# Two input column blocks side by side while x arrives, with the squares of x, the constants and eight extra matmuls moved to go with it

## The chip, the cores and the metric

One core of a Trainium2 chip runs the whole program. The time is the device time of one execution in microseconds. Each kernel is run several times; the median counts. A further execution is taken with the hardware profiler; the rows below come from it.

## What is computed

One transformer block on 512 tokens of width 2048, in float32: a norm, one wide input projection, a state-space mixer and a sparse-attention mixer side by side, an output projection, and a gated feed-forward layer of width 5632 with a last norm.

```python
def rmsnorm(x, w):
    xf = xf * lax.rsqrt(jnp.mean(xf * xf, axis=-1, keepdims=True) + NORM_EPS)
    return xf.astype(x.dtype) * w
...
u = rmsnorm(h, attn_norm_w[l])
z, xbc, dt_raw, q, kc, vc, ks, vs, kw, vw, gate_raw = jnp.split(u @ w_in[l], split_at, axis=-1)
y_ssd = ssd_mixer(z, xbc, dt_raw, ...)
y_att = nsa_mixer(q, kc, vc, ks, vs, kw, vw, gate_raw, ...)
h = h + jnp.concatenate([y_ssd, y_att], axis=-1) @ w_out[l]
v = rmsnorm(h, ffn_norm_w[l])
h = h + (jax.nn.silu(v @ w_gate[l]) * (v @ w_up[l])) @ w_down[l]
return rmsnorm(h, final_norm_w)
```

The change concerns the first norm and the first two of the 41 column blocks of `u @ w_in`.

## The kernel before

**Layout.** Everything is held transposed: features lie on the 128 partitions, the 512 tokens along a row. x is 16 row blocks of 128 features (`xt`, KD = 16), each 128 x 512.

**A product of float32 accuracy** is three fast matmuls. Weight and operand are each split into a high part (rounded by a copy on ScalarE) and a low part (the rest, on VectorE); TensorE adds high x high, high x low and low x high into one PSUM bank (lines 254, 255 and 256). For u the high part is ScalarE's copy of x times the norm's gain, and the low part one VectorE operation with two multiplied and subtracted operands (line 1955). The norm's scale, 1/rms of each token, is not in u: it is multiplied in later, when a finished column block is read from PSUM (`rrow`).

**A column block** of the input projection is a `Unit`: 16 row blocks, 48 matmuls of 512 columns into one bank. Its weights come in four transfers of four row blocks each, 256 KB (`subs`). `issue_dma` starts a transfer into one of four `raw` buffers, `issue_split` makes the high part (`whi`, four buffers), `issue_low` the low part (`wlo`, four buffers). `run_unit` runs one block after another, with splits three transfers ahead (LEAD). The banks: two `ps_t` for the first two blocks, two `ps_s` for the next two, two `ps_g` from then on. A block is read out ("evacuated") by VectorE with `rrow`, so none is read before the norm's sums are through; from the seventh block on, a block starts only when the one two before it has been read.

**The start.** SP's queue takes the transfers in order: a weight transfer, x's first row block, the gains (`colc`), then the rest of x with a weight transfer after every second transfer of x, then the constants (`ident` for transposes, `tri`, the large table of masks and rotation angles in `kc`). The squares of x are taken in the same stretch: even row blocks on ScalarE with the sum added up on GpSimd, odd ones squared and added on VectorE; then the two sums are added. `rms_stats` lets TensorE sum over the partitions by four matmuls with ones (line 306), takes the power on GpSimd and spreads the result by four transposes (line 316).

**What sets the order.** Up to the output projection a scheduler orders each engine's instructions by its own simulated timeline, within what the data allow. From the feed-forward layer on the order is written in the program (`manual_schedule`). On the chip every engine takes its list in order and waits on semaphores.

Of the kernel before, what the change touches and what calls it, by code (L numbers as in the profile page):

```python
# [29 lines left out]
LEAD = 3  # L30
# [81 lines left out]
def body(ctx, tc, xT, w_in, w_out, w_gate, w_up, w_down, w1k, w1v, cols, rows, kst, out):  # L112
    nc = tc.nc
    act, dve, pool, pe = nc.scalar, nc.vector, nc.gpsimd, nc.tensor
    sch = Sched()

    def f(ap):
        return ap.bitcast(F32)

    def a_hi(dst, src, scale=1.0):  # L120
        act.activation(dst, src, AF.Copy, scale=scale)  # L121
# [4 lines left out]
    def mul(eng, o, a, b):  # L126
        eng.tensor_tensor(o, a, b, ALU.mult)

    def add(eng, o, a, b):
        eng.tensor_tensor(o, a, b, ALU.add)  # L130
# [20 lines left out]
    def ps_m():  # L151
        return ps("m", 1)
# [30 lines left out]
    subs = []  # L183
# [9 lines left out]
                subs.append((src[:, k:k + n, :], n))  # L193

    st = {"dma": 0, "split": 0, "low": 0}
    raw, hi_t, lo_t = {}, {}, {}

    def issue_dma(upto):
        while st["dma"] <= min(upto, len(subs) - 1):
            i = st["dma"]  # L200
            src, n = subs[i]
            raw[i] = wp.tile([128, KSUB, 128], F32, tag="raw", name="wraw", bufs=4)
            nc.sync.dma_start(raw[i][:, :n, :], src)
            st["dma"] += 1
# [25 lines left out]

    U_LAST = NU + KD + 2

    def run_unit(u):
        if u.pre:
            u.pre()
        if u.need:
            sch.run_until(*u.need)
        n_u = st["unit"] = st.get("unit", 0) + 1
        if n_u > 6:
            sch.run_until(("evac", n_u - 2))  # L240
        p = ps_t() if n_u <= 2 or n_u > U_LAST + 2 else ps_s() if n_u <= 4 or U_LAST < n_u <= U_LAST + 2 else ps_g()
        p = p[:, 0:u.cols[1] - u.cols[0]]
        unit_of[id(p)] = n_u
        for i, k0, n in u.sub:
            issue_low(i)
            for j in range(n):
                if j == 0:
                    issue_split(i + LEAD)
                if j == 2:
                    issue_low(i + LEAD)  # L250
                k = k0 + j
                ah, al = [t[:, u.cols[0]:u.cols[1]] for t in u.rhs(k)]
                with tc.issue_after(R["pv"].ins) if u.late else nullcontext():
                    pe.matmul(p, hi_t[i][:, j, :], ah, start=(k == 0), stop=False)  # L254
                    pe.matmul(p, hi_t[i][:, j, :], al, start=False, stop=False)  # L255
                    pe.matmul(p, lo_t[i][:, j, :], ah, start=False, stop=(k == u.nk - 1))  # L256
                sch.tick()
                if u.hook:
                    u.hook(k)
            del hi_t[i], lo_t[i]  # L260

        def evac():
            yield 1
            yield from u.evac(p)
            assert ("evac", n_u) in sch.flags
            del unit_of[id(p)]
        sch.add(evac())


    colc = cst.tile([128, C_W2 + 4], F32, name="colc")  # L270
    nhalf = colc[:, C_W2:C_W2 + 4]
    ones = cst.tile([128, 128], F32, name="ones")
    ident = cst.tile([128, 128], F32, name="ident")
# [14 lines left out]
    def kcs(a, n):  # L288
        return kc[:, a - K_TRI:a - K_TRI + n]

    tri = kcs(K_TRI, 128)
# [4 lines left out]
    def col(c, n=1):  # L296
        return colc[:, c:c + n]
# [1637 lines left out]

    xs = open_pool("xs")
    xt = xs.tile([128, KD, 512], F32, name="xt")
    issue_dma(0)
    nc.sync.dma_start(xt[:, 0, :], xT[0])
    nc.sync.dma_start(colc[:, 0:C_PE], cols[:, 0:C_PE])  # L1940
    nc.sync.dma_start(xt[:, 1, :], xT[1])
    for k in range(2, KD, 2):
        nc.sync.dma_start(xt[:, k:k + 2, :], xT[k:k + 2].rearrange("k p t -> p k t"))
        if k % 4 == 2:
            issue_dma(k // 4 + 1)
    nc.gpsimd.dma_start(rowc, rows.to_broadcast([128, 48]))
    dve.memset(ones, 1.0)
    act.activation(nhalf, ones[:, 0:4], AF.Copy, scale=-0.5)
    for k in range(KD):
        if k % 4 == 0:  # L1950
            issue_low(k // 4)
        t = xt[:, k, :]
        w = col(C_AN + k)
        a_hi(u_hi[:, k, :], t, scale=w)
        dve.scalar_tensor_tensor(u_lo[:, k, :], t, w, f(u_hi[:, k, :]), op0=ALU.mult, op1=ALU.subtract)
    acc1 = acc2
    accb = xs.tile([128, 512], F32, name="accb")
    for k in range(KD):
        t = xt[:, k, :]
        if k < 2:  # L1960
            act.activation((acc1, accb)[k], t, AF.Square)
        else:
            sq = xs.tile([128, 512], F32, tag=f"sq{k % 2}", name="sq", bufs=2)
            if k % 2:
                mul(dve, sq, t, t)
                add(dve, accb, accb, sq)
            else:
                act.activation(sq, t, AF.Square)
                add(pool, acc1, acc1, sq)
    add(dve, acc1, acc1, accb)  # L1970
    nc.sync.dma_start(ident, kst[:, 0:K_TRI])
    nc.sync.dma_start(tri, kst[:, K_TRI:K_AM])
    close_pool("xs")
    open_pool("kcp")
    open_pool("ssd")
# [4 lines left out]
    first = units[0].evac  # L1980

    def ev_first(p):
        yield from rms_stats(acc1, D, rrow, "r1")
        yield from first(p)
    units[0].evac = ev_first
    for n, u in enumerate(units):
        if n == 4:
            nc.sync.dma_start(kcs(K_AM, NK - K_AM), kst[:, K_AM:NK])
            nc.sync.dma_start(colc[:, C_PE:C_W2], cols[:, C_PE:C_W2])
# [98 lines left out]
```

## Time and profile before

| | us |
|---|---|
| timed runs | 2243.98, 2245.19, 2245.45 (median 2245.19) |
| the profiled execution | 2247.26 |
| its span, first to last instruction | 2245.5 |
| mean granted clock of TensorE | 0.99 |
| DMA | 419.57 MB, 187 GB/s on average |

The span of the profile is cut into windows or listed by instruction; times in it count from its start. A matmul's printed duration overlaps the next matmul's, since they are pipelined: the distance from one start to the next is the cost. PE is TensorE, PEld its weight loads, DVE VectorE, ACT ScalarE, POOL GpSimd, SP the queue that issues most transfers. `ps_t<-u,whi` means: writes a bank `ps_t`, reads u and a weight's high part.

### The profile page before, as it was taken

The numbers are of one execution on the slowest core, as the hardware profiler recorded it, in microseconds if no ns is written. First come the engines' busy times: TensorE is split into PE (matmuls) and PEld (weight loads), VectorE is DVE, ScalarE is ACT, GpSimd is POOL, SyncE is SP. The second block draws the span as 40 slices with busy tenths as digits, with TensorE's granted clock in tenths as the row PEclk, the third lists the DMA queues.
The fourth block names the chain that finished last, engine by engine and source line by source line (L and its number), as shares of the span: only waits on it lengthen the run. The fifth ranks groups of instructions, "written<-read, shape, count | busy, mean of one in ns | idle before, by whom it ended". The sixth has DMA issues, their size and how long they took to land.

```text
span 2245.5 us, 39743 instructions
## 1 busy us (share of the span) xinstructions
PE 2176.5 (97%) x15376; PEld 2028.3 (90%) x15376; DVE 1811.8 (81%) x2912; ACT 1092.1 (49%) x1767; POOL 430.5 (19%) x440
## 2 busy tenths in 40 slices
PE   7999999999999999999999999999999899999996
PEld 5888888888888778999999999999999799999995
DVE  7698777788788777888888888888788887877886
ACT  4564456667666644444444444444444343333353
POOL 2011234333233133000000000000001221112132
PEclk9999999999999999999999999999999999999998
DMA  5222352222435165878788787878876867878775
GB/s 179 91 74 76 115 171 92 88 87 73 153 128 154 54 230 156 247 219 242 215 255 228 227 235 214 251 225 245 229 219 223 327 206 256 252 248 254 218 176 142
DMA packets 153645, 419.57 MB, mean 187 GB/s; under 512 B 16512, under 2 KB 24720, under 8 KB 153456
## 3 DMA queue, kind: packets, MB, share of 16 engines
q1 hardware_dynamic: 99712, 252.63, 32.7%
q0 software_dynamic: 25456, 77.37, 17.7%
q10 hardware_dynamic: 28288, 87.04, 11.1%
q8 instruction: 120, 1.97, 0.4%
q14 instruction: 69, 0.57, 0.1%
HBM read 353.54 MB, written 59.51 MB: 184 GB/s over the span
## 4 chain that ended last, share of the span: by engine, by line
PE 86%; DVE 6%; DMA 4%; issue 2%; ACT 1%; POOL 0%; ACTq 0%; DVEq 0%; POOLq 0%; SPq 0%
PE ps_g L254 8%; PE ps_g L256 8%; PE ps_g L255 8%; PE ps_t L1363 6%; PE ps_g L1363 6%; PE ps_g L1362 6%; PE ps_g L1361 6%; PE ps_t L1361 6%; PE ps_s L1363 6%; PE ps_t L1362 6%; PE ps_s L1361 6%; PE ps_s L1362 6%; DVE R L124 2%; PE ps_v L984 2%; PE ps_t L957 1%
## 5 line engine op out<-in xcount | busy, mean ns | idle before, releaser
L121 ACT ACTIVATE R<-Z 128x1024 fp32r<-128x1024 f32 (+5 forms) x477 | 433.4, 926 | 542.5 <-DVE Z L130 304.8
L124 DVE TENSOR_TENSOR R<-Z,R 128x1024 fp32r<-128x1024 f32 (+5 forms) x371 | 386.2, 1047 | 28.8 <-ACT R L121 22.2
L254 PE MATMUL ps_g<-u,whi 128*128 128x512 f32 x736 | 293.1, 399 | 0.0
L256 PE MATMUL ps_g<-u,wlo 128*128 128x512 f32 x736 | 290.6, 395 | 0.0
L255 PE MATMUL ps_g<-u,whi 128*128 128x512 f32 x736 | 289.4, 393 | 0.2 <-DVE u L124 0.2
L1361 PE MATMUL ps_s<-u,R 128*128 128x256 f32 (+1 forms) x747 | 215.4, 288 | 1.7 <-ACT R L121 1.7
L1362 PE MATMUL ps_s<-u,R 128*128 128x256 f32 (+1 forms) x747 | 214.9, 288 | 0.0
L1361 PE MATMUL ps_g<-u,R 128*128 128x256 f32 (+1 forms) x748 | 213.8, 286 | 0.2 <-ACT R L121 0.2
L1362 PE MATMUL ps_g<-u,R 128*128 128x256 f32 (+1 forms) x748 | 213.2, 285 | 0.0
L1361 PE MATMUL ps_t<-u,R 128*128 128x256 f32 (+1 forms) x705 | 202.0, 287 | 0.2 <-ACT R L121 0.2
L1362 PE MATMUL ps_t<-u,R 128*128 128x256 f32 (+1 forms) x705 | 201.6, 286 | 0.0
L124 DVE TENSOR_TENSOR wlo<-wraw,whi 128x512 fp32r<-128x512 f32 x200 | 158.4, 794 | 52.5 <-ACT whi L121 51.6
L121 ACT ACTIVATE whi<-wraw 128x512 fp32r<-128x512 f32 x200 | 125.3, 627 | 144.0 <-PE ps_g L255 97.4
L1363 PE MATMUL ps_g<-u,R 128*128 128x256 f32 (+1 forms) x620 | 177.9, 287 | 2.3 <-DVE R L124 2.2
L1363 PE MATMUL ps_s<-u,R 128*128 128x256 f32 (+1 forms) x595 | 170.3, 286 | 2.5 <-DVE R L124 2.5
L256 PEld LDWEIGHTS ps_g<-u,wlo 128*128 128x128 f32 x736 | 138.5, 188 | 27.4
L255 PEld LDWEIGHTS ps_g<-u,whi 128*128 128x128 f32 x736 | 138.7, 188 | 26.4 <-DVE u L124 0.5
L254 PEld LDWEIGHTS ps_g<-u,whi 128*128 128x128 f32 x736 | 138.7, 188 | 25.6 <-ACT e L121 0.2
L1361 PEld LDWEIGHTS ps_s<-u,R 128*128 128x128 f32 x747 | 140.5, 188 | 4.1 <-ACT R L121 2.1
L1362 PEld LDWEIGHTS ps_s<-u,R 128*128 128x128 f32 x747 | 141.0, 189 | 2.2
L1361 PEld LDWEIGHTS ps_g<-u,R 128*128 128x128 f32 x748 | 140.7, 188 | 1.8 <-ACT R L121 0.4
L1362 PEld LDWEIGHTS ps_g<-u,R 128*128 128x128 f32 x748 | 141.0, 189 | 1.5
(470 smaller groups left out, 6436.4 us busy)
## 6 DMA issues: line engine op xcount, KB each, us to landing
Z<-in_w_gate SPq DMA_DIRECT2D x95, 512.0 KB, 5.3
Z<-in_w_up SPq DMA_DIRECT2D x93, 512.0 KB, 7.3
wraw<-in_w_in SPq DMA_DIRECT2D x164, 256.0 KB, 3.0
g_d<-A ACTq DMA_DIRECT2D x22, 1792.0 KB, 7.4
Z<-in_w_down SPq DMA_DIRECT2D x59, 384.0 KB, 6.0
u<-g_d ACTq DMA_DIRECT2D x11, 1792.0 KB, 8.7
Z<-in_w_gate POOLq DMA_DIRECT2D x35, 512.0 KB, 7.5
Z<-in_w_up POOLq DMA_DIRECT2D x35, 512.0 KB, 5.6
```

The lines of the kernel that those rows point to most:

```text
L121: act.activation(dst, src, AF.Copy, scale=scale)
L124: eng.tensor_tensor(dst, src, f(hi), ALU.subtract)
L254: pe.matmul(p, hi_t[i][:, j, :], ah, start=(k == 0), stop=False)
L255: pe.matmul(p, hi_t[i][:, j, :], al, start=False, stop=False)
L256: pe.matmul(p, lo_t[i][:, j, :], ah, start=False, stop=(k == u.nk - 1))
L957: pe.transpose(p[:, kb * 128:(kb + 1) * 128], e[:, kb * 128:(kb + 1) * 128], ident)
L984: R["pv"] = pe.matmul(o[:, kb * 128:512], v[:, kb, br, :], rhs, start=False, stop=(br == 1 and kb == 3 and t is tl))
L1361: pe.matmul(q, h[:, k, :], ah, start=(k == 0), stop=False)
L1362: pe.matmul(q, h[:, k, :], al, start=False, stop=False)
L1363: pe.matmul(q, l[:, k, :], ah, start=False, stop=(k == s.blk.n - 1))
```

## The change

It does five things.

1. The first two column blocks run side by side: the weight transfers of the two are taken in turn, and after every four row blocks of x come the 12 matmuls of the one and the 12 of the other. `run_unit` is cut into `start_unit`, `run_sub` and `end_unit` for that; for the other blocks nothing changes in it.
2. The weight transfers are placed between those of x at other points, six of them ahead of x's end instead of four.
3. All squares of x are taken on ScalarE and added up on VectorE into one sum, and both stand behind that engine's last split of u. GpSimd has no part in it.
4. Constants are loaded later, behind the weight transfers issued so far (`issue_after` sets only the order on the queue).
5. Eight matmuls of ones by ones, 128 x 128, go to TensorE ahead of everything; their result is not read.

```diff
-    raw, hi_t, lo_t = {}, {}, {}
+    raw, hi_t, lo_t, raw_dma = {}, {}, {}, []
...
-            nc.sync.dma_start(raw[i][:, :n, :], src)
+            raw_dma.append(nc.sync.dma_start(raw[i][:, :n, :], src))
...
+    def run_unit(u):
+        p, n_u = start_unit(u)
+        for sub in u.sub:
+            run_sub(u, p, sub)
+        end_unit(u, p, n_u)
...
+    pair = units[0:2]
+    subs[0:8] = [subs[4 * (i % 2) + i // 2] for i in range(8)]
+    for a, u in enumerate(pair):
+        u.sub = [(2 * g + a, k, n) for g, (_, k, n) in enumerate(u.sub)]
     issue_dma(0)
     nc.sync.dma_start(xt[:, 0, :], xT[0])
     nc.sync.dma_start(colc[:, 0:C_PE], cols[:, 0:C_PE])
+    issue_dma(1)
     nc.sync.dma_start(xt[:, 1, :], xT[1])
     for k in range(2, KD, 2):
+        if k > 2:
+            issue_dma(k // 2)
         nc.sync.dma_start(xt[:, k:k + 2, :], xT[k:k + 2].rearrange("k p t -> p k t"))
-        if k % 4 == 2:
-            issue_dma(k // 4 + 1)
...
-    for k in range(KD):
-        if k % 4 == 0:
-            issue_low(k // 4)
...
-        a_hi(u_hi[:, k, :], t, scale=w)
-        dve.scalar_tensor_tensor(u_lo[:, k, :], t, w, f(u_hi[:, k, :]), op0=ALU.mult, op1=ALU.subtract)
-    acc1 = acc2
-    accb = xs.tile([128, 512], F32, name="accb")
+    warm = ps_m()
+    for _ in range(8):
+        pe.matmul(warm[:, 0:128], ones, ones, start=True, stop=True)
+    p0 = [start_unit(u) for u in pair]
+    for g in range(4):
+        for k in range(4 * g, 4 * g + 4):
+            if k % 4 < 2:
+                issue_low(2 * g + k % 4)
+            t = xt[:, k, :]
+            w = col(C_AN + k)
+            last_hi = act.activation(u_hi[:, k, :], t, AF.Copy, scale=w)
+            last_lo = dve.scalar_tensor_tensor(u_lo[:, k, :], t, w, f(u_hi[:, k, :]), op0=ALU.mult, op1=ALU.subtract)
+        for u, (p, _) in zip(pair, p0):
+            run_sub(u, p, u.sub[g])
     for k in range(KD):
         t = xt[:, k, :]
-        if k < 2:
-            act.activation((acc1, accb)[k], t, AF.Square)
-        else:
-            sq = xs.tile([128, 512], F32, tag=f"sq{k % 2}", name="sq", bufs=2)
-            if k % 2:
-                mul(dve, sq, t, t)
-                add(dve, accb, accb, sq)
-            else:
-                act.activation(sq, t, AF.Square)
-                add(pool, acc1, acc1, sq)
-    add(dve, acc1, acc1, accb)
-    nc.sync.dma_start(ident, kst[:, 0:K_TRI])
-    nc.sync.dma_start(tri, kst[:, K_TRI:K_AM])
+        with tc.issue_after(last_hi.ins):
+            if k:
+                sq = xs.tile([128, 512], F32, tag=f"sq{k % 2}", name="sq", bufs=2)
+            act.activation(sq if k else acc2, t, AF.Square)
+        with tc.issue_after(last_lo.ins):
+            if k:
+                add(dve, acc2, acc2, sq)
+    with tc.issue_after(raw_dma[-1].ins):
+        nc.sync.dma_start(ident, kst[:, 0:K_TRI])
+        nc.sync.dma_start(tri, kst[:, K_TRI:K_AM])
...
+            with tc.issue_after(raw_dma[-1].ins):
+                nc.sync.dma_start(kcs(K_AM, NK - K_AM), kst[:, K_AM:NK])
+                nc.sync.dma_start(colc[:, C_PE:C_W2], cols[:, C_PE:C_W2])
```

What the scheduler makes of it is seen in three places. The numbers behind the names tell buffers apart.

TensorE in the kernel before, where the second column block (bank `ps_t_301`) first appears, after 36 matmuls of the first (`ps_t_234`):

```order
L256 MATMUL ps_t_234<-u_95,wlo_150 128x512
L254 MATMUL ps_t_234<-u_95,whi_162 128x512
L254 MATMUL ps_t_301<-u_95,whi_247 128x512
L255 MATMUL ps_t_301<-u_95,whi_247 128x512
L255 MATMUL ps_t_234<-u_95,whi_162 128x512
L256 MATMUL ps_t_234<-u_95,wlo_164 128x512
```

TensorE now, from its first instruction (first block `ps_t_139`, second `ps_t_140`):

```order
L1967 MATMUL ps_m_130<-ones_77 128x128 x8
L257 MATMUL ps_t_139<-u_95,whi_141 128x512
L257 MATMUL ps_t_140<-u_95,whi_147 128x512
L258 MATMUL ps_t_139<-u_95,whi_141 128x512
L259 MATMUL ps_t_139<-u_95,wlo_143 128x512
L258 MATMUL ps_t_140<-u_95,whi_147 128x512
L259 MATMUL ps_t_140<-u_95,wlo_149 128x512
```

The second block has moved from the 37th place to the second: both blocks use a row block of x as soon as it is there. The norm's sums (lines 306 before, 316 now) stand after 90 of the 512-column matmuls before and after 151 now.

ScalarE before, around the last split of x and behind it (`u` is a split, `sq` a square, `whi` a weight's high part):

```order
L121 ACTIVATE whi_162<-wraw_115 128x512
L121 ACTIVATE u_95<-xt_100,colc_76 128x512 x2
L1968 ACTIVATE sq_209<-xt_100 128x512
L121 ACTIVATE u_95<-xt_100,colc_76 128x512 x2
L1968 ACTIVATE sq_215<-xt_100 128x512
L121 ACTIVATE whi_247<-wraw_119 128x512
L121 ACTIVATE whi_265<-wraw_152 128x512
```

ScalarE now, at the same place; `whi_219` and `whi_245` are the high parts of the last four row blocks of the two first column blocks:

```order
L1975 ACTIVATE u_95<-xt_100,colc_76 128x512 x2
L121 ACTIVATE whi_201<-wraw_118 128x512
L1975 ACTIVATE u_95<-xt_100,colc_76 128x512 x6
L1984 ACTIVATE acc2_96<-xt_100 128x512
L1984 ACTIVATE sq_326<-xt_100 128x512
L1984 ACTIVATE sq_329<-xt_100 128x512
L1984 ACTIVATE sq_332<-xt_100 128x512
L1984 ACTIVATE sq_335<-xt_100 128x512
L121 ACTIVATE whi_219<-wraw_121 128x512
L121 ACTIVATE whi_245<-wraw_124 128x512
L121 ACTIVATE whi_263<-wraw_211 128x512
```

The squares have moved from between the splits of x to behind them, five of them ahead of the two high parts.

SP's queue before, from its first transfer:

```order
L203 DMA wraw_101<-in_w_in 128x512
L1939 DMA xt_100<-in_xT 128x512
L1940 DMA colc_76<-in_cols 128x116
L1941 DMA xt_100<-in_xT 128x512
L1943 DMA xt_100<-in_xT 128x2x512
L203 DMA wraw_107<-in_w_in 128x512
L1943 DMA xt_100<-in_xT 128x2x512 x2
L203 DMA wraw_111<-in_w_in 128x512
```

SP's queue now:

```order
L203 DMA wraw_101<-in_w_in 128x512
L1954 DMA xt_100<-in_xT 128x512
L1955 DMA colc_76<-in_cols 128x116
L203 DMA wraw_105<-in_w_in 128x512
L1957 DMA xt_100<-in_xT 128x512
L1961 DMA xt_100<-in_xT 128x2x512
L203 DMA wraw_109<-in_w_in 128x512
L1961 DMA xt_100<-in_xT 128x2x512
```

A second weight transfer stands ahead of x's second row block, and weights and x then alternate one to one.

More of the change, by code (lines that the diff above doesn't have):

```diff
@@ L231, in body, with start_unit @@
     U_LAST = NU + KD + 2
-    def run_unit(u):
+    def start_unit(u):
         if u.pre:
@@ L243, in run_unit, with run_sub, end_unit @@
         unit_of[id(p)] = n_u
[L244 to L260, printed above, removed]
+        return p, n_u
+    def run_sub(u, p, sub):
+        i, k0, n = sub
+        issue_low(i)
+        for j in range(n):
+            if j == 0:
+                issue_split(i + LEAD)
+            if j == 2:
+                issue_low(i + LEAD)
+            k = k0 + j
+            ah, al = [t[:, u.cols[0]:u.cols[1]] for t in u.rhs(k)]
+            with tc.issue_after(R["pv"].ins) if u.late else nullcontext():
+                pe.matmul(p, hi_t[i][:, j, :], ah, start=(k == 0), stop=False)
+                pe.matmul(p, hi_t[i][:, j, :], al, start=False, stop=False)
+                pe.matmul(p, lo_t[i][:, j, :], ah, start=False, stop=(k == u.nk - 1))
+            sch.tick()
+            if u.hook:
+                u.hook(k)
+        del hi_t[i], lo_t[i]
+    def end_unit(u, p, n_u):
         def evac():
@@ L1937, in body @@
     xt = xs.tile([128, KD, 512], F32, name="xt")
+    pair = units[0:2]
+    assert [i for u in pair for i, _, _ in u.sub] == list(range(8))
+    subs[0:8] = [subs[4 * (i % 2) + i // 2] for i in range(8)]
+    for a, u in enumerate(pair):
+        u.sub = [(2 * g + a, k, n) for g, (_, k, n) in enumerate(u.sub)]
     issue_dma(0)
@@ L1948, in body @@
     act.activation(nhalf, ones[:, 0:4], AF.Copy, scale=-0.5)
-    for k in range(KD):
-        if k % 4 == 0:
-            issue_low(k // 4)
-        t = xt[:, k, :]
-        w = col(C_AN + k)
-        a_hi(u_hi[:, k, :], t, scale=w)
-        dve.scalar_tensor_tensor(u_lo[:, k, :], t, w, f(u_hi[:, k, :]), op0=ALU.mult, op1=ALU.subtract)
-    acc1 = acc2
-    accb = xs.tile([128, 512], F32, name="accb")
+    warm = ps_m()
[12 more added lines that the diff above has]
+            run_sub(u, p, u.sub[g])
     for k in range(KD):
         t = xt[:, k, :]
-        if k < 2:
-            act.activation((acc1, accb)[k], t, AF.Square)
-        else:
-            sq = xs.tile([128, 512], F32, tag=f"sq{k % 2}", name="sq", bufs=2)
-            if k % 2:
-                mul(dve, sq, t, t)
-                add(dve, accb, accb, sq)
-            else:
-                act.activation(sq, t, AF.Square)
-                add(pool, acc1, acc1, sq)
-    add(dve, acc1, acc1, accb)
-    nc.sync.dma_start(ident, kst[:, 0:K_TRI])
-    nc.sync.dma_start(tri, kst[:, K_TRI:K_AM])
+        with tc.issue_after(last_hi.ins):
[8 more added lines that the diff above has]
+        nc.sync.dma_start(tri, kst[:, K_TRI:K_AM])
     close_pool("xs")
@@ L1982, in ev_first @@
     def ev_first(p):
-        yield from rms_stats(acc1, D, rrow, "r1")
+        yield from rms_stats(acc2, D, rrow, "r1")
         yield from first(p)
     units[0].evac = ev_first
+    for u, (p, n_u) in zip(pair, p0):
+        end_unit(u, p, n_u)
     for n, u in enumerate(units):
         if n == 4:
-            nc.sync.dma_start(kcs(K_AM, NK - K_AM), kst[:, K_AM:NK])
-            nc.sync.dma_start(colc[:, C_PE:C_W2], cols[:, C_PE:C_W2])
+            with tc.issue_after(raw_dma[-1].ins):
+                nc.sync.dma_start(kcs(K_AM, NK - K_AM), kst[:, K_AM:NK])
+                nc.sync.dma_start(colc[:, C_PE:C_W2], cols[:, C_PE:C_W2])
+        if n < 2:
+            continue
         if order.index(first_att) <= n < len(units) - 1:
```

## The prediction

> **What bounds the kernel now.** First the page's busy times, then the first 40 us in windows, then who waited there, then the matmuls one by one.
>
> ```profile
> span 2245.5 us, 39743 instructions
> PE 2176.5 (97%) x15376; PEld 2028.3 (90%) x15376; DVE 1811.8 (81%) x2912; ACT 1092.1 (49%) x1767; POOL 430.5 (19%) x440
> ```
> ```profile
> 0.00:10.00 10.00, 3.07 (x6) 2.10 (x7) 3.85 (x7) 6.43 (x11) 0.93 (x5) 1.00 0.78 245
> 10.00:20.00 10.00, 4.70 (x11) 2.15 (x9) 10.00 (x9) 10.00 (x18) 6.85 (x5) 0.84 1.06 391
> 20.00:30.00 10.00, 8.00 (x20) 5.67 (x21) 10.00 (x13) 3.19 (x7) 2.70 (x2) 0.67 0.21 75
> 30.00:40.00 10.00, 9.70 (x40) 7.30 (x40) 9.09 (x17) 2.57 (x5) 0.00 (x0) 0.98 0.42 135
> ```
> ```profile
> PEld ps_t L255 <- DVE u L1955: 12.2, 9, 3.4
> ```
> TensorE is the bound of the whole kernel (97%). It is not so in the first 34 us: there it starts at most 37 matmuls in 30 us, and its weight loads wait for VectorE's low parts of u (12.2 us in nine waits). VectorE is full from 10 to 30 us. The windows' columns are PE, PEld, DVE, ACT, POOL, granted clock, DMA share, GB/s.
>
> ```profile
> 6.93 0.79 PE L254 MATMUL ps_t<-u,whi 128*128 128x512 f32 x1 [6.93 <-ACT u L121]
> 8.73 0.63 PE L254 MATMUL ps_t<-u,whi 128*128 128x512 f32 x1
> 9.16 0.63 PE L255 MATMUL ps_t<-u,whi 128*128 128x512 f32 x1
> ...
> 35.95 0.39 PE L254 MATMUL ps_t<-u,whi 128*128 128x512 f32 x1
> ...
> 43.20 0.39 PE L256 MATMUL ps_t<-u,wlo 128*128 128x512 f32 x1
> 43.43 0.95 PE L306 MATMUL ps_m<-ones,acc 128*128 128x1 f32 x8
> 44.23 0.48 PE L254 MATMUL ps_t<-u,whi 128*128 128x512 f32 x1
> ...
> 45.69 0.39 PE L254 MATMUL ps_s<-u,whi 128*128 128x512 f32 x1
> ```
> Between 35.95 and 43.20 us stand 32 matmul periods: 0.2266 us each at full clock. At 8.73 and 9.16 they are 0.43 us apart: half clock. The first two column blocks are 2 x 16 x 3 = 96 matmuls; they end where ps_s begins, at 45.69. Without the norm's sums (43.43 to 44.23, 0.80 us), which the change moves behind them, that is 44.89. At the full pace 96 take 21.75 us; from 6.93 they would end at 28.7. So 16.2 us are lost in this stretch, and that is all that can be won there if the first matmul doesn't come earlier.
>
> **What the change does to the stretch.** Durations first: the start's groups of instructions, then three low-part splits beside GpSimd and three after it.
>
> ```profile
> L1955 DVE SCALAR_TENSOR_TENSOR u<-xt,colc,u 128x512 fp32r<-128x512 f32 x16 | 15.4, 996 | 0.6 <-ACT u L121 0.6
> L121 ACT ACTIVATE u<-xt,colc 128x512 fp32r<-128x512 f32 x16 | 10.6, 710 | 0.1
> L130 POOL TENSOR_TENSOR acc<-acc,sq 128x512 f32<-128x512 f32 x7 | 9.6, 1365 | 11.9 <-ACT sq L1968 11.9
> L121 ACT ACTIVATE whi<-wraw 128x512 fp32r<-128x512 f32 x11 | 6.9, 626 | 19.0 <-PE ps_t L255 10.3 <-DMA wraw<-in_w_in 5.2 <-issue 2.0
> L1968 ACT ACTIVATE sq<-xt 128x512 f32<-128x512 f32 x7 | 4.3, 615 | 0.0
> ```
> ```profile
> 18.25 4.10 DVE L1955 SCALAR_TENSOR_TENSOR u<-xt,colc,u 128x512 fp32r<-128x512 f32 x3
> 22.17 1.32 POOL L130 TENSOR_TENSOR acc<-acc,sq 128x512 f32<-128x512 f32 x1 [0.37 <-ACT sq L1968]
> 25.17 2.06 DVE L1955 SCALAR_TENSOR_TENSOR u<-xt,colc,u 128x512 fp32r<-128x512 f32 x3
> 24.57 0.68 DVE L124 TENSOR_TENSOR wlo<-wraw,whi 128x512 fp32r<-128x512 f32 x1
> ```
> Three splits take 4.10 us beside GpSimd's adds and 2.06 us once these are over. The change removes GpSimd's seven adds, and puts VectorE's squares and adds behind the last split. VectorE's 16 splits of u and six of weights then take 16 x 0.69 + 6 x 0.62 = 14.8 us (paces from the last two rows: 2.06/3, and 25.17 - 24.57 plus a little). Fifteen VectorE operations go and fifteen adds come: no more work for it, but later.
>
> ```profile
> 6.15 1.35 ACT L121 ACTIVATE u<-xt,colc 128x512 fp32r<-128x512 f32 x2
> 8.13 1.03 SPq L1943 DMA_DIRECT2D xt<-in_xT  x2
> ```
> ```profile
> xt<-in_xT SPq DMA_DIRECT2D x1, 512.0 KB, 9.6
> ```
> *Transfers.* Weight block, x and gains come first on SP's queue, as before, so the first split starts at 6.15 and the first matmul at 6.93 again. The last x was issued at about 8.8 and landed 9.6 us later, at 18.4, with four weight blocks on the queue ahead of it. Now six are ahead; two more of 0.262 MB at 391 GB/s (row of 10 to 20 us) are 1.3 us: 19.7. The seventh and eighth weight blocks, issued behind all of x, land at 20.4 and 21.1. ScalarE follows x: its last split ends at 21.1, VectorE's at 21.9.
>
> *TensorE.* With two blocks side by side each row block of x feeds 6 matmuls, 1.36 us at full clock, and a row block arrives every 0.8 us (fifteen between about 7.4 and 19.7). So after the first three or four row blocks TensorE is the bound, not the splits. I laid the steps out in the program's order with these durations. If the clock were full from the first matmul, TensorE would wait 1.7 us for data and end the 96 at 30.4. If it stays at half until 13.4 us, almost no wait is left and the end is 31.9; early half clock falls where data is short anyway. I take **31.1**, between the two, against 44.89: **13.8 us gained**, with ends of 14.5 and 13.0.
>
> *Waits on the way.* On ScalarE the fifth block's high part waits for a buffer that TensorE frees after 24 matmuls, at 13 to 16 us, with ten splits of x queued behind it; it is due at 14.3, so they slip by 1.5 us at most, and TensorE has 24 more matmuls to do meanwhile. On SP the fifth block's transfer waits for VectorE's first low part (6.3 us) with x behind it, which is before its turn. One place has no cover: ScalarE takes five squares (5 x 0.615 = 3.1 us) ahead of the high part of the seventh weight block, so that is ready at 24.8 and its low part at 25.5. TensorE reaches row block 12 at 31.1 - 24 x 0.2266 = 25.7. It is just in time; each us that the squares slip costs one.
>
> ```profile
> 0.84 0.17 DVE L1947 MEMSET ones<- 128x128 f32 x1 [0.84 <-PEq L2080]
> 49.99 0.60 PE L316 MATMUL ps_m<-ident,rst 128*128 128x128 f32 x4
> ```
> *Eight matmuls of ones* start at 1.0, when ones are set. No row shows this operation. The nearest, four fp32 transposes of the same size, take 0.60 us, about 0.11 each from one to the next; an fp32 matmul leaves two records (L306: 4 issued, x8), so eight are 1.8 us at full and 3.5 at half clock, over by 4.6. At double that they would end at 8.1 and hold the first matmul for 1.2 us; if they bring the clock up at once they win 0.7 against my 31.1. I take nothing.
>
> The granted clock, in the window where it was lowest:
> ```profile
> 16.78:23.61 6.83, 3.96 (x10) 2.79 (x9) 6.83 (x5) 5.93 (x12) 4.99 (x4) 0.50 0.70 257
> ```
> TensorE is busy 3.96 of these 6.83 us, and all of it runs at half clock. After the change no such hole is left in the start. [...]
>
> *Constants late.* ident, tri and the large table leave SP's queue ahead of the weights. Ident and tri now stand behind weight block 14, issued by about 35 us, and are first needed by the transposes, at about 49 us; the large table (0.85 MB, 2.2 us at 391 GB/s) stands behind weight block 22 and serves stages that come much later. Cover: a DMA share of 0.2 to 0.4. Cost nothing; at worst 2.2 us once.
>
> **What stands behind the stretch.** The norm's sums now stand after 151 matmuls, not 90, so at 31.1 + 55 x 0.2266 = 43.6 us: the same time as before. Their input is the last of 15 adds, two of which queue behind a weight split that waits for a weight buffer TensorE frees at 36.5: ready at about 39. Slack 4 us. So rrow comes at about 50 us again, and all evacuations start then, while TensorE is 61 matmuls further. Six PSUM banks hold blocks 0 to 5; block 6 starts at about 76 (31.1 + 192 x 0.2266 + 1.5 for the small matmuls between) and needs block 4 read.
>
> ```profile
> sum 70.00, PE 70.00 PEld 57.98 DVE 50.27 ACT 36.04 POOL 0.00; mean PE 10.00 PEld 8.28 DVE 7.18 ACT 5.15 POOL 0.00
> ```
> ```profile
> 40.00:240.00 200.00, 200.00 (x1008) 167.52 (x1007) 167.40 (x343) 99.74 (x155) 22.12 (x16) 1.00 0.24 80
> 240.00:440.00 200.00, 198.34 (x1041) 168.57 (x1041) 139.41 (x316) 115.22 (x241) 68.70 (x85) 1.00 0.38 124
> 440.00:640.00 200.00, 200.00 (x1081) 172.33 (x1080) 164.33 (x432) 135.99 (x320) 65.58 (x69) 1.00 0.32 107
> 760.00:800.00 40.00, 33.21 (x144) 25.01 (x143) 23.37 (x64) 21.45 (x50) 2.06 (x3) 0.87 0.29 96
> ```
> VectorE had 50.3 us of work in the 70 us from 50 to 120 (first row, the windows' sum), 19.7 idle. Now 56 us must do: 5.9 idle are left. From 40 to 640 TensorE was never idle but for 1.7 us, and VectorE and ScalarE have idle time in every 200 us, so an earlier TensorE should stay earlier. From about 410 us the engines' order is the same, apart from a few rows near 790. I take the gain as kept whole.
>
> **Sum.** The profiled execution took 2247.26 us (span 2245.5): 2247.26 - 13.8 = 2233.5. The three timed runs have a median of 2245.19, 2.07 lower; the forecast on that scale is **2231.4**. A measurement of this kernel tells about 0.2%, 4.5 us, from no change.
>
> **Rivals.**
> 1. *The clock is up at once* (ones): end at 30.4, and with no slip elsewhere a us more: 2230. [...] Chance 0.10.
> 2. *VectorE's backlog takes half back.* For it: the evacuations start no earlier, and only 5.9 us of slack are left before 106 us. Against: no wait of TensorE at all in 40 to 240. If VectorE needs 5 to 8 us more there, TensorE waits for a PSUM bank once: 2237 to 2240. Chance 0.14.
> 3. *It does not do what it says*: the attention's own chain ends the first phase. In 760 to 800 TensorE is busy 33.2 of 40 us; if what it waits for there hangs on VectorE and ScalarE from 50 us on, an earlier TensorE only waits longer: 2243 to 2246. Against: these engines idle in every window. Chance 0.08.
> 4. *Slower*: VectorE runs from 50 to 120 us at the pace it has beside GpSimd and becomes the bound there.
>
> ```profile
> 140.00:160.00 20.00, 20.00 (x108) 16.96 (x107) 20.00 (x44) 12.18 (x18) 1.60 (x2) 1.00 0.24 79
> 160.00:180.00 20.00, 20.00 (x102) 16.68 (x101) 19.81 (x31) 9.66 (x16) 7.50 (x5) 1.00 0.25 80
> ```
> With GpSimd busy 7.5 us instead of 1.6, a full VectorE finishes 31 instructions instead of 44: 1.42 times slower. Its 50.3 us would become 71.4, 15.4 more than the 56 there are, 1.6 more than the gain. TensorE would then stop for long enough to lose its clock; two windows of 6.83 us at half clock are 6.8 us more: up to 2254, say 2251. It decides from 69.8 us of VectorE work in that stretch (1.39 times). Against: GpSimd has nothing between 50 and 106 us in the changed order. Chance 0.05.
>
> **Numbers.** The forecast (2230.5 to 2232.5) has 0.62, rival 1 0.10, rival 2 0.14, rival 3 0.09, rival 4 0.05. Faster by over 0.2%: 0.62 + 0.10 + 0.14 = 0.86; same 0.09; slower 0.05. The range holds the forecast and rivals 1 and 2, with a us for the spread of runs: 2228.5 to 2239.5; 0.14 is left out.
>
> **What would show it.** Right: the first 512-wide matmul at 6.9 us, six matmuls of one row block in a row, ps_s from 30.5 to 32; VectorE's splits all near 0.7 us; the norm's sums at 42 to 45 us; no TensorE waits to 240 us. Wrong: the burst ending past 6.9; ScalarE's seventh high part later than 25.7 and TensorE waiting for it; waits of TensorE on VectorE's evacuations at 70 to 110 us; a TensorE idle for longer than 7 us in 745 to 790.

## The result, and the profile after

The changed kernel takes **2233.1 us** (median of 4 runs, 2230.1 to 2234.8) against 2245.3 for the kernel before it (4 runs, 2244.0 to 2245.9): ratio 0.9941, 95% interval 0.9928 to 0.9953. Measured again on another occasion it took 2234.78 against 2246.12: 0.9950, 0.9936 to 0.9963. The profiled execution took 2233.11 us; that of before took 2247.26, 2 us above its median, so the two profiles lie further apart than the medians.

The page's span and busy times, after:

```profile
span 2231.3 us, 39774 instructions
PE 2174.8 (97%) x15392; PEld 2029.9 (91%) x15392; DVE 1806.5 (81%) x2912; ACT 1090.2 (49%) x1770; POOL 427.6 (19%) x433
```

The engines' busy times are those of before to within 6 us; the span is 14.2 us shorter. Idle time has gone, not work. The windows of the start, after (PE, PEld, DVE, ACT, POOL, granted clock, DMA share, GB/s):

```profile
0.00:10.00 10.00, 7.46 (x30) 5.93 (x30) 3.38 (x6) 5.37 (x8) 0.93 (x5) 1.00 0.75 229
10.00:20.00 10.00, 9.67 (x42) 7.40 (x41) 8.90 (x14) 8.35 (x15) 0.00 (x0) 1.00 1.05 390
20.00:30.00 10.00, 9.20 (x41) 7.15 (x40) 9.45 (x16) 9.69 (x19) 0.00 (x0) 1.00 0.39 137
30.00:40.00 10.00, 10.00 (x46) 8.29 (x45) 8.66 (x16) 6.03 (x12) 0.00 (x0) 1.00 0.49 156
```

From 10 to 30 us TensorE does 83 matmuls where it did 31, and GpSimd does nothing. Then the timeline of the start, after (start, length, engine, line; in brackets the idle time before it and what ended it):

```profile
1.06 3.79 PE L1967 MATMUL ps_m<-ones 128*128 128x128 f32 x16 [1.06 <-DVE ones L1963]
6.19 1.13 PE L257 MATMUL ps_t<-u,whi 128*128 128x512 f32 x2 [1.35 <-ACT u L1975]
7.16 0.40 PE L258 MATMUL ps_t<-u,whi 128*128 128x512 f32 x1
7.39 0.39 PE L259 MATMUL ps_t<-u,wlo 128*128 128x512 f32 x1
...
18.74 4.13 DVE L1976 SCALAR_TENSOR_TENSOR u<-xt,colc,u 128x512 fp32r<-128x512 f32 x6
...
22.47 2.18 ACT L1984 ACTIVATE sq<-xt 128x512 f32<-128x512 f32 x4
...
24.55 1.66 ACT L121 ACTIVATE whi<-wraw 128x512 fp32r<-128x512 f32 x3
...
25.22 0.50 PE L257 MATMUL ps_t<-u,whi 128*128 128x512 f32 x1 [0.80 <-ACT whi L121]
...
43.34 0.95 PE L316 MATMUL ps_m<-ones,acc 128*128 128x1 f32 x8
```

Six low-part splits take 4.13 us, 0.69 each; beside GpSimd three took 4.10. The last low part ends at 22.88 us (33.56 before). The first two column blocks have 96 matmuls; the 97th of the 512-column matmuls starts at 30.88 (44.89 before, the norm's sums left out): 14.0 us. This point is called the end of the 96 below. In the change the scheduler put two `ps_s` matmuls of the third block ahead, from 28.61 on, so the pair itself is through at 31.33. Matmuls stand 0.23 us apart from 7.16 on, where they were 0.43 apart at 8.73 in before: here the clock is full from the first real ones (granted in full from 5.44 us). The row at 25.22 is the one place that the prediction left without cover: five squares on ScalarE (the four at 22.47 and one before them) ahead of a weight's high part, 0.80 us of wait.

Where this gain stands later is read from fixed points: the 2,400 matmuls of the first phase's column blocks (L257 to L259; L254 to L256 before), counted from the last. The 750th from the last starts at 490.4 us (502.0 before), the 300th at 657.3 (668.8), the last at 778.6 (790.2). So 11.6 us of the 14.0 are kept to the first phase's end.

All kernels of this study, from their one profile each (us from the span's start), with medians of the timed runs; each ratio is to runs of before that were measured beside that kernel:

| kernel | last low part of u | 96 matmuls end | 750th | 300th | last | median | ratio to before, 95% |
|---|---|---|---|---|---|---|---|
| before | 33.56 | 44.89 | 502.0 | 668.8 | 790.2 | 2245.3 | |
| the change | 22.88 | 30.88 | 490.4 | 657.3 | 778.6 | 2233.1 | 0.9928–0.9953 |
| squares_back | 35.28 | 40.17 | 497.2 | 669.3 | 789.1 | 2247.3 | 0.9999–1.0018 |
| one_by_one | 21.29 | 35.04 | 492.0 | 658.9 | 780.0 | 2238.8 | 0.9948–0.9978 |
| no_ones | 22.51 | 30.51 | 488.0 | 654.8 | 776.2 | 2230.8 | 0.9912–0.9942 |
| const_early | 23.07 | 32.08 | 489.0 | 655.8 | 776.3 | 2233.1 | 0.9922–0.9955 |
| changed_again | 22.43 | 31.35 | 491.0 | 657.8 | 777.7 | 2234.8 | 0.9936–0.9963 |
| hi_first | 22.48 | 31.49 | 490.7 | 657.7 | 779.5 | 2236.2 | 0.9944–0.9968 |
| hi_first_no_ones | 22.77 | 30.75 | 489.0 | 656.0 | 775.5 | 2232.6 | 0.9927–0.9953 |
| squares_late_old | 23.11 | 33.69 | 490.7 | 658.0 | 779.3 | 2239.9 | 0.9957–0.9981 |
| all_on_vector | 28.74 | 33.61 | 490.7 | 658.8 | 778.4 | 2238.2 | 0.9946–0.9974 |
| all_on_gpsimd | 36.13 | 43.53 | 502.1 | 668.9 | 789.9 | 2247.8 | 0.9999–1.0019 |
| late_gpsimd | 23.03 | 31.25 | 492.4 | 665.1 | 784.3 | 2245.1 | 0.9987–1.0006 |
| squares_mid | 26.70 | 31.88 | 490.4 | 661.4 | 782.9 | 2239.3 | 0.9951–0.9979 |

### The profile page after: what moved, and what is told of

Its sections match the earlier page's. It is cut to its first block, busy times and chain, and to the rows that moved or that the text cites. A ratio compares the mean times of both kernels' runs of the same rounds, so it can differ in the third digit from the quotient of the medians.

```text
span 2231.3 us, 39774 instructions
## 1 busy us (share of the span) xinstructions
PE 2174.8 (97%) x15392; PEld 2029.9 (91%) x15392; DVE 1806.5 (81%) x2912; ACT 1090.2 (49%) x1770; POOL 427.6 (19%) x433
## 4 chain that ended last, share of the span: by engine, by line
PE 83%; DVE 8%; DMA 4%; issue 2%; ACT 1%; POOL 1%; SPq 0%; ACTq 0%; DVEq 0%; POOLq 0%
PE ps_g L258 7%; PE ps_g L257 7%; PE ps_g L259 7%; PE ps_t L1373 6%; PE ps_g L1373 6%; PE ps_t L1371 6%; PE ps_t L1372 6%; PE ps_g L1372 6%; PE ps_g L1371 6%; PE ps_s L1373 6%; PE ps_s L1371 6%; PE ps_s L1372 6%; DVE R L124 2%; PE ps_v L994 2%; PE ps_t L967 1%
## 5 line engine op out<-in xcount | busy, mean ns | idle before, releaser
L124 DVE TENSOR_TENSOR R<-Z,R 128x1024 fp32r<-128x1024 f32 (+5 forms) x371 | 391.1, 1059 | 28.2 <-ACT R L121 17.8
L257 PE MATMUL ps_g<-u,whi 128*128 128x512 f32 x736 | 292.5, 398 | 0.7 <-DVE h L127 0.7
L259 PE MATMUL ps_g<-u,wlo 128*128 128x512 f32 x736 | 290.7, 395 | 0.0
L259 PEld LDWEIGHTS ps_g<-u,wlo 128*128 128x128 f32 x736 | 138.7, 188 | 27.1
L257 PEld LDWEIGHTS ps_g<-u,whi 128*128 128x128 f32 x736 | 138.8, 189 | 26.8 <-ACT pth L121 1.1
```

Source lines behind the costliest of these rows:

```text
L124: eng.tensor_tensor(dst, src, f(hi), ALU.subtract)
```

## The experiments

Each kernel is the changed one with the edit shown, and each does the whole computation.

**The four parts, each undone alone.** First the squares:

```diff
-        with tc.issue_after(last_hi.ins):
...
-            act.activation(sq if k else acc2, t, AF.Square)
-        with tc.issue_after(last_lo.ins):
-            if k:
-                add(dve, acc2, acc2, sq)
+        if k < 2:
+            act.activation((acc2, accb)[k], t, AF.Square)
...
+            if k % 2:
+                mul(dve, sq, t, t)
+                add(dve, accb, accb, sq)
+            else:
+                act.activation(sq, t, AF.Square)
+                add(pool, acc2, acc2, sq)
+    add(dve, acc2, acc2, accb)
```


> The changed kernel with the squares of x taken as before, between the splits: even row blocks on ScalarE and GpSimd, odd ones on VectorE. Theory A (the squares were what held the splits; moving them is the larger part of the gain): VectorE again does its squares and adds between the splits and runs at half pace beside GpSimd's adds, its last low part of u comes at 33 to 36 us and not at 22.8, and the 96 matmuls of the first two blocks end at 36 to 38 us and not at 30.9: 5 to 7 us slower than the changed kernel, 2238 to 2240. Theory B (setting two blocks side by side is the gain, the squares are hidden by it): the 96 end by 33 and the time is within 2 us of the changed kernel.

The 96 matmuls end 9.3 us later than in the change, at 40.17 and not at 36 to 38. VectorE's splits of x in the change, in the groups of 6 to 45 us:

```profile
L1976 DVE SCALAR_TENSOR_TENSOR u<-xt,colc,u 128x512 fp32r<-128x512 f32 x16 | 11.3, 749 | 3.0 <-ACT u L1975 2.9
```

and VectorE's splits and GpSimd's adds in squares_back:

```profile
L1976 DVE SCALAR_TENSOR_TENSOR u<-xt,colc,u 128x512 fp32r<-128x512 f32 x16 | 14.6, 940 | 1.4 <-ACT u L1975 1.4
L130 POOL TENSOR_TENSOR acc<-acc,sq 128x512 f32<-128x512 f32 x7 | 11.2, 1599 | 13.2 <-ACT sq L1990 13.1
```

A split takes 940 ns on average, against 749 in the change. One by one they are of two kinds: thirteen take 0.74 to 0.75 us, as in the change, and three, all beside a GpSimd add, 1.77 to 1.86. VectorE's squares and their adds stand in the way besides. But the end tells a second thing: of the 4.7 us that this kernel still wins in the start (44.89 to 40.17), 4.8 are there at 490 us and none at 657. Its time is that of before, and not 2238 to 2240. Something between these points costs it 5 us, and that is taken up below.

The pair undone, with the weight transfers placed as before:

```diff
-        for u, (p, _) in zip(pair, p0):
-            run_sub(u, p, u.sub[g])
+        run_sub(pair[0], p0[0][0], pair[0].sub[g])
+    for sub in pair[1].sub:
+        run_sub(pair[1], p0[1][0], sub)
```


> The changed kernel with the first two blocks one after the other again and the weight transfers placed as before; squares late, constants late and ones stay. Theory A: the first block follows x and ends at about 21 us; the second then waits for a high part that stands behind five squares on ScalarE, until 23.5, and ends 10.9 us later: 34 to 35 us against 30.9, so 3 to 4 us slower than the changed kernel, 2236 to 2237. Theory B: without the pair most of the 14 us are lost; the 96 end beyond 38 us and the time is 2241 or more.

The end of the 96 moves by 4.2 us, to 35.04, though the low parts are ready earlier (21.29): with one block at a time TensorE cannot use the row blocks as fast as they come. By 22 us it has started 48 matmuls of 512 columns; the change has started 63 and its repeat (changed_again), with a late clock, 55. Then it waits 1.5 us for a high part that stands behind five squares, as expected. The median is 5.7 us above that of the change; of the 4.2 us, 1.6 are left at the 750th matmul from the last.

The ones and the constants:

```diff
-    warm = ps_m()
-    for _ in range(8):
-        pe.matmul(warm[:, 0:128], ones, ones, start=True, stop=True)
```


> The changed kernel without the eight matmuls of ones. Theory A (they bring the clock up before the first real matmul; in the changed kernel the full clock was granted from 5.44 us): the first matmuls run at half clock, 0.43 us apart, until somewhere between 10 and 14 us; early half clock falls where data are short, so the 96 end at 31 to 32.5 and not at 30.9: 0 to 1.5 us slower. Theory B (the clock would be up anyway, or half clock at the start costs its whole length): either no row at half clock at all, or 3 us and more.


```diff
-    with tc.issue_after(raw_dma[-1].ins):
-        nc.sync.dma_start(ident, kst[:, 0:K_TRI])
+    nc.sync.dma_start(ident, kst[:, 0:K_TRI])
...
-            with tc.issue_after(raw_dma[-1].ins):
-                nc.sync.dma_start(kcs(K_AM, NK - K_AM), kst[:, K_AM:NK])
+            nc.sync.dma_start(kcs(K_AM, NK - K_AM), kst[:, K_AM:NK])
```


> The changed kernel with the constants not held back: ident, tri and the large table then stand on SP's queue between the last of x and the seventh weight block. Theory A: the seventh block lands 2.5 us later, at about 22.9, still ahead of its turn on ScalarE (24.5), and the eighth at about 24.3 against 25.1: no more than 0.5 us slower, not to be told from the changed kernel. Theory B (late constants are worth their transfer time): TensorE waits 2.5 us longer for the last row blocks, the 96 end at 33.4.

Neither brings a gain that can be told from nothing. Without the ones the 96 end at 30.51, sooner than the 31 to 32.5 expected, and the median is 2.3 us lower. Leaving them out also changes the later order (from the 660th place of VectorE's list on, about 190 places differ from the change's, nearly all before 630 us), so the 2.3 us, small as they are, can't be put to the ones alone. With early constants both medians are 2233.1.

**The wait that was left.** The squares are held behind the high parts of weight blocks 7 and 8 (their adds behind the low parts); the second kernel leaves out the ones too. They ran beside the changed kernel on one chip.

```diff
-        with tc.issue_after(last_hi.ins):
+        with tc.issue_after(w_hi[7].ins):
-        with tc.issue_after(last_lo.ins):
+        with tc.issue_after(w_lo[7].ins):
```


> The changed kernel as it is, again, as the companion of the next three on one chip. 2233 us; first two blocks end near 31 (30.9 to 32.1 by when the clock comes up); TensorE waits about 0.9 us at 24 to 25 for the high part of the seventh weight block.

> Squares stand behind the high parts of weight blocks 7 and 8, their adds behind the low parts, instead of behind the last splits of x. Theory (the five squares ahead of that high part are the only uncovered cost of the change): the wait at 24 to 25 goes, ScalarE has both high parts done by 23.5, the first two blocks end 0.9 us earlier at the same clock (about 30), time 2232. Rival (TensorE is bound there by something else, or the squares come out later and hold the norm's sums): no gain, 2233 to 2235, sums later than 43.5.

> As the one before, without the eight matmuls of ones. Theory (the burst brings nothing that lasts, and the scheduler's order at 600 to 900 us that came with leaving it out is worth a us or two): 2229 to 2231, first two blocks end at 29.5 to 30.5. Rival (the burst pays when it lifts the clock early): 2233 to 2234, the blocks end a us later than with it.

ScalarE now does the high parts first, as ordered. Its timeline in hi_first:

```profile
21.55 1.14 ACT L213 ACTIVATE whi<-wraw 128x512 fp32r<-128x512 f32 x2
22.59 0.62 ACT L1985 ACTIVATE acc<-xt 128x512 f32<-128x512 f32 x1
```

In these profiles there was nothing to win. The repeat of the changed kernel has no wait at 25 us either; there the clock came up late. Its TensorE timeline:

```profile
6.37 1.47 PE L257 MATMUL ps_t<-u,whi 128*128 128x512 f32 x2 [1.53 <-ACT u L1975]
7.63 0.63 PE L258 MATMUL ps_t<-u,whi 128*128 128x512 f32 x1
8.06 0.63 PE L259 MATMUL ps_t<-u,wlo 128*128 128x512 f32 x1
...
12.97 0.39 PE L259 MATMUL ps_t<-u,wlo 128*128 128x512 f32 x1
```

The matmuls stand 0.43 us apart until 12.7, TensorE comes to the last row blocks later, when the high parts are ready, and its 96 end at 31.35, only 0.47 us behind the profile with the early clock. It looks as if the half clock of the start and this wait hide each other. That is not shown: in both kernels with the high parts first the clock came up late (12.8 and 11.5 us), so none was rid of both. hi_first's time (2236.2) and that of changed_again (2234.8) cannot be told apart; the expectation of a us less was not borne out. The norm's sums came at 46.45 us instead of 43.8, as the rival said, and TensorE did not wait for them. Again the kernel without ones is the lower of its pair, by 3.6 us, and again it has the later order of no_ones.

**Place or engine?** The change does two things to the squares: it holds them back, and it frees GpSimd of the adds. Each alone:

In squares_late_old the loop of before stands inside the change's two holds:

```diff
         with tc.issue_after(last_hi.ins):
...
+                if k % 2 == 0:
+                    act.activation(sq, t, AF.Square)
...
         with tc.issue_after(last_lo.ins):
+                if k % 2:
+                    mul(dve, sq, t, t)
+                    add(dve, accb, accb, sq)
+                else:
+                    add(pool, acc2, acc2, sq)
```

all_on_vector is squares_back with one word changed, and all_on_gpsimd has all squares on ScalarE and all fifteen adds on GpSimd, not held back:

```diff
-                add(pool, acc2, acc2, sq)
+                add(dve, acc2, acc2, sq)
```
```diff
+        act.activation(sq if k else acc2, t, AF.Square)
+        if k:
+            add(pool, acc2, acc2, sq)
```


> The squares on the engines of before (seven squares and eight adds on VectorE, seven adds on GpSimd), but put behind the last splits as in the changed kernel. Theory A (the place is what counts): last low part at 22.9 and the first two blocks end at 31 to 32, as in the changed kernel; GpSimd's adds slow VectorE from 23 us on, which TensorE's four weight buffers hide: 2233 to 2235. Rival (taking GpSimd out is what counts): VectorE's low parts of the weights come late beside GpSimd, TensorE waits for them from 25 to 35 us, the blocks end at 33 to 35, 2236 to 2239.

> As squares_back (squares among the splits, all else of the change kept), but GpSimd's seven adds are done by VectorE: 13 square operations stand ahead of its last low part instead of 11. Theory (GpSimd beside VectorE is what doubles VectorE's time): 16 + 6 + 13 operations at 0.69 us from 6.4, so the last low part ends at about 30.6 instead of 35.3, the first two blocks at about 35.5 instead of 40.2; 2237 to 2239. Rival (only VectorE's number of operations counts): last low part at 36 to 37, blocks end at 41, no faster than 2245.

> As squares_back, but ScalarE squares and GpSimd makes all fifteen adds: VectorE has nothing but splits in the start. Theory (GpSimd beside VectorE is what doubles its time): VectorE's 22 splits still take about 1.37 us each while GpSimd adds, so the last low part ends at 32 to 35 and the first two blocks at 36 to 39; 2238 to 2242. Rival (the number of VectorE's operations counts): the last low part follows ScalarE at 27 to 28, blocks end at 32 to 33, 2234 to 2235.

VectorE's and GpSimd's groups in the start of all_on_gpsimd:

```profile
L130 POOL TENSOR_TENSOR acc<-acc,sq 128x512 f32<-128x512 f32 x15 | 23.3, 1554 | 10.3 <-ACT sq L1983 9.3
L1976 DVE SCALAR_TENSOR_TENSOR u<-xt,colc,u 128x512 fp32r<-128x512 f32 x16 | 21.5, 1386 | 2.0 <-ACT u L1975 2.0
```

and of all_on_vector:

```profile
L1976 DVE SCALAR_TENSOR_TENSOR u<-xt,colc,u 128x512 fp32r<-128x512 f32 x16 | 11.5, 746 | 1.3 <-ACT u L1975 1.3
L130 DVE TENSOR_TENSOR acc<-acc,sq 128x512 f32<-128x512 f32 x7 | 4.8, 685 | 0.0
```

This settles what slows the splits. With all adds on GpSimd, VectorE has nothing but splits to do, and is the slowest of all: 1386 ns a split, last low part at 36.1, beyond the 32 to 35 that were expected; the 96 end at 43.53, beyond 36 to 39, and the time, 2247.8, is beyond 2238 to 2242. The mean is again one of two kinds: ten splits take 1.75 to 1.78 us and six 0.74 to 0.79, with nothing between. With GpSimd's seven adds given to VectorE on top of its own, it is back to 746 ns, and its last low part ends 6.5 us earlier than in squares_back (28.74 and 35.28), although two more operations stand ahead of it. Holding back alone also spares the splits: in squares_late_old the last low part ends at 23.11, as in the change. But GpSimd's adds then run beside the weights' low parts, and TensorE waits 2.5 us for those (1.5 the longest), which the four weight buffers were expected to hide: 33.69 and 2239.9, about the rival's numbers.

```profile
PE ps_t L259 <- DVE wlo L124: 2.5, 2, 1.5
```

**The 5 us that squares_back lost.** The work from about 60 us on is interleaved by the kernel's scheduler, and it answers to the start. Between before and the change, VectorE's instructions differ in many of the first 640 places (up to 404 us) and then agree but for 11 rows. squares_back has another order for the attention: from the 660th place on, 569 places differ from the change's, nearly all before 761 us. Two more kernels get that order, late_gpsimd (the change with its held-back adds on GpSimd) and squares_mid (the change with nothing held back); neither has squares_back's slow start.

```diff
         with tc.issue_after(last_lo.ins):
             if k:
-                add(dve, acc2, acc2, sq)
+                add(pool, acc2, acc2, sq)
```
```diff
-        with tc.issue_after(last_hi.ins):
...
-        with tc.issue_after(last_lo.ins):
-            if k:
-                add(dve, acc2, acc2, sq)
+        if k:
+            add(dve, acc2, acc2, sq)
```


> The changed kernel with its fifteen late adds on GpSimd. The start should be that of the changed kernel (last low part 22.9, first two blocks end at 31), the norm's sums at 43.5 to 45. But the scheduler gives it the order of attention that squares_back has (from about 90 us on) in place of the changed kernel's. Theory (squares_back lost its 4.7 us of the start to that order at 550 to 670 us): the last 512-wide matmul of the first phase starts at 781 to 783 instead of 776 to 778.6, and the time is 2236 to 2239. Rival (that loss has nothing to do with the order): 2231 to 2234.

> The changed kernel with its squares and adds no longer held behind the splits, so that they stand among them; GpSimd has no adds. The scheduler again gives it the order of attention that squares_back and late_gpsimd have. Start: ten adds ahead of VectorE's last low part, 32 operations of 0.69 us from 6.4, so it ends at 28 to 29 and the first two blocks at 33 to 34, as in all_on_vector. Theory (the order costs 5 to 6 us by itself): from the 750th to the 300th of the last 2,400 matmuls it takes 172 to 173 us, not 167; the last one starts at 784 to 786, and the time is 2239 to 2244. Rival (late_gpsimd lost it by its late adds on GpSimd, squares_back by its start): 167 us, the last at 778 to 780, time 2234 to 2238 as all_on_vector.

From the 750th to the 300th matmul from the last it takes 172.2 us in squares_back, 172.7 in late_gpsimd and 170.9 in squares_mid; in before and the change 166.8 and 166.9, and in the nine others 166.7 to 168.1. squares_mid shows it best, since it stands at 490.4 us exactly where the change stands, with GpSimd out of the start; its loss is a little under the 5 to 6 us expected (170.9 and not 172 to 173, the last matmul at 782.9 and not 784 to 786). TensorE's waits from 600 to 666 us in the change:

```profile
PE ps_s L924 <- DVE em L934: 2.1, 1, 2.1
PE ps_v L994 <- ACT pth L121: 0.6, 1, 0.6
```

and in squares_mid:

```profile
PE ps_s L924 <- DVE em L934: 4.0, 5, 1.7
PE ps_v L994 <- DVE ptl L124: 0.4, 1, 0.4
PE ps_v L994 <- ACT pth L121: 0.3, 1, 0.3
PE ps_v L986 <- DVE at L130: 0.2, 1, 0.2
```

One wait for VectorE's masks has become five. The waits shown explain 2.2 of the 4.0 us; squares_back and late_gpsimd have 3.4 us more at half clock in the same stretch, too, which is 1.7 us. late_gpsimd lost more than was expected (2245.1, not 2236 to 2239): 5.7 us of it at the first phase's end, the rest behind it, where its second phase took 6.2 us longer than the change's. That part isn't explained by any experiment here.

## Why the prediction was right, step by step

The forecast was 2231.4 us; it is 2233.1, inside the range and on the side forecast.

- **The stretch.** 96 matmuls to end at 31.1: 30.88, 31.35 when repeated. The two ends, 30.4 with the clock up at once and 31.9 with half clock until 13.4 (13.37 in before), proved too far apart: the profiles with full clock from 5.44 and from 12.71 us lie 0.47 apart, since the early one loses 0.80 us behind the squares. That the middle between them was hit owes something to luck: the early end was put 0.5 us too early and the late one as much too late. The sign "ps_s from 30.5 to 32" did not come out: two such matmuls stand at 28.61, the rest from 31.33 on.
- **Transfers.** The first matmul was to start at 6.93 again. It starts at 6.19 to 6.78 in the change, its repeat and no_ones (6.18 to 6.98 in all 14 profiles), so up to 0.7 us of the 14.0 in this profile are of that kind. The last transfer of x lands at 20.7 and not at 19.7, and the last low part ends at 22.9, a us later than worked out; nobody waits for it.
- **VectorE.** "No more work for it, but later" and the pace of 0.69 us held. The sum did not part the two causes, and the runs do. From 44.89, the pair (with the ones and the constants) gives 4.7 us (squares_back, 40.17), GpSimd's adds moved to VectorE 6.6 (all_on_vector, 33.61), VectorE's squares moved to ScalarE 1.7 (squares_mid, 31.88), and holding them back 0.5 to 1.0 (the change). In the other order, holding the old squares back first, that alone gives 6.5 (squares_late_old, 33.69): the two overlap, since either keeps GpSimd's adds from VectorE's splits. Each step may be off by some 0.5 us, since the clock came up at different times (0.47 us lie between the change and its repeat).
- **The place without cover.** Foretold as just in time; a wait of 0.80 us in one profile and none in the other. Putting the high parts first brings nothing that the medians show.
- **VectorE's backlog.** The sum left VectorE 5.9 us idle from 50 to 106 us. In the change it is busy 41.6 of these 56 us, so 14.4 are idle: not all the work of 50 to 120 us in before falls into this stretch, and TensorE waits for no evacuation there. The slack was sized too small. Rival 4 had no ground either: GpSimd does nothing from 50 to 120 us (its factor of 1.42 came from two windows with different instructions). That a stop there would cost the clock was an estimate: before is at half clock from 16.78 and from 661.90 us, behind stops of 2.44 and 2.13 us, while in the change TensorE is busy all 70 us from 50 to 120. Of the rivals' chances, rival 3 has 0.08 where it is told and 0.09 in the sum.
- **The ones** were put at no gain: right. The two kernels without them have the two lowest medians, 2.3 and 3.6 us below their companions, but with overlapping intervals and another later order. The burst ends at 4.85, worked out as 4.6. Rival 1's condition, a clock that is up at once, came true in the profile of the change, but in only 2 of 11 profiles with the burst, and in one of these two the clock fell back to half from 8.4 to 11.8 us.
- **The constants:** nothing, as said.
- **The norm's sums** at 43.6: 43.34, with no wait of TensorE there.

**"I take the gain as kept whole"** is the step that was off, by 2.4 us. At the 1,500th matmul from the last the gain is 12.9 us (268.8 to 255.9): the change has TensorE wait 0.7 us for VectorE between 45 and 312 us, where before it never waited; this is the sign "no TensorE waits to 240 us" that failed, at 206 us:

```profile
PE ps_t L537 <- DVE pf L563: 0.5, 1, 0.5
PE ps_t L538 <- DVE ml L124: 0.2, 1, 0.2
```

Behind the 1,350th another 1.5 go. The windows from there to the 1,200th, before:

```profile
311.00:356.70 45.70, 44.04 (x249) 37.46 (x248) 28.76 (x48) 21.65 (x47) 24.89 (x29) 1.00 0.36 112
```

and after:

```profile
298.10:345.30 47.20, 45.54 (x248) 38.66 (x247) 28.65 (x48) 22.47 (x48) 25.63 (x30) 0.96 0.35 108
```

The idle time is the same 1.66 us, with as many matmuls, but the clock is 0.96 instead of 1.00: 3.41 us at half clock, half of which is lost. At the 750th, the 300th and the last matmul the gain is 11.4 to 11.6 us, about what the medians show (12.2 and 11.3 us).

This second loss need not be the change's own. Twelve of the 14 profiles have the same 1.66 us of idle time there, and only four of them fall to half clock behind it: the change, its repeat, all_on_gpsimd and squares_mid. So the same wait costs 1.7 us more in one profile than in another, and one profile of before can't tell what that kernel does on the whole.

The reason given for keeping it, that the order from 410 us on is the same, was the weightiest sentence of the prediction, and it is a condition and not a rule. It held for this change (11 rows differ from 404 us on). Where it doesn't hold, 4 to 6 us go. None of the rivals was this: the wait at 206 us is for VectorE, as rival 2 had it, but for an operand and not for a bank, and no rival named the clock at 320 us or another order.

squares_late_old and all_on_vector end the start 2.7 to 2.8 us behind the change and yet stand beside it at 490 us (490.7); one_by_one, 4.2 us behind, is 1.6 behind there. All three are without the change's wait at 206 us and without its half clock at 320 us, 0.7 and 1.7 us, which makes up 2.4 us of each. What stays open is the rest of the way: squares_late_old and all_on_vector are still beside the change at the last matmul (779.3 and 778.4), while their medians are 3 to 7 us above it. One profile is too little there: all_on_vector's was the fastest of its seven runs, 2233.2 with a median of 2238.2. The second phase alone takes 1451.6 to 1458.9 us in the 14 profiles.

## What to carry to other kernels

Look first at what runs on GpSimd beside a VectorE that feeds TensorE: here it won 6.5 us of the start to keep seven GpSimd adds from the time in which VectorE split, either by holding them back or by letting VectorE do them itself, more than the order of the blocks (4.2 with 1.5 of it behind the squares, 4.7 with the ones, the constants and the weight transfers). Where a scheduler interleaves later work, compare the later order before and after an early edit, since an order that changes by accident can cost as much as the edit wins. A short wait that one profile shows may be gone in the next, when the clock comes up at another time (0.80 us in the change, none in its repeat); it is not yet a gain.

## What the runs showed of the hardware

- **GpSimd's adds more than double the VectorE splits that they catch.** A split takes 0.74 to 0.75 us alone. In all_on_gpsimd, with GpSimd adding nearly throughout, ten of sixteen take 1.75 to 1.78 us; the mean, 1386 ns, only counts how many were caught. GpSimd's own adds take 1.29 us with VectorE idle (the first of late_gpsimd, at 23.3 us) and 1.60 to 1.62 us for twelve of the fifteen in all_on_gpsimd, but 1.29 to 1.44 us in before, beside a VectorE that is full from 10 to 30 us. A split grows in one step and not by degrees: none of these sixteen lies between 0.79 and 1.75 us. What holds it up inside the chip is not shown.
- **The same burst brought the clock up early in two profiles of eleven.** The same eight matmuls at 1.06 to 4.85 us had the clock full from 4.99 (all_on_vector) and 5.44 us (the change) in two profiles and from 9.6 to 12.8 in nine. Without them it was full from 9.74 (no_ones), 11.51 (hi_first_no_ones) and 13.37 us (before). Later stretches at half clock in before and the change last 3.41, 6.83 or 10.24 us, but for the last, which runs to the program's end. How busy TensorE was over 3.41 us does not tell where the clock comes up: it was busy 3.26 of the 3.41 us to 4.99 in all_on_vector and 2.81 of the 3.41 to 5.44 in the change, with the clock full from there on; but also 2.93 of the 3.41 to 9.30 in changed_again and 3.03 of the 3.41 to 9.96 in before, where it was full only 3.41 us later. The ends of matmuls are modelled, so these sums are rough. What decides is not shown.
- The windows' clock column says 1.00 for the first microseconds in every profile, before the first record of the throttle, even where the matmuls stand 0.43 us apart (in before 1.00 from 0 to 13.36 us, with 0.43 from 8.73 to 9.16). There the distance of matmuls is the clock.
